# Hybrid decoder step on one core: embedding weights split ahead and a fixed order at the two norm steps

## The chip, the core and the metric

The kernel runs on 1 core of one Trainium2 chip. The metric is device time in microseconds (us). Engines are named as in the profile: PE does matmuls (PEld its weight loads), DVE is the vector engine, ACT the scalar engine, POOL the general engine, SP the queue that starts the transfers.

## The reference, cut to what matters

One layer is computed for 288 positions at once (256 of a prompt, 32 of a sample group), with 2048 features. After the attention and the gated mixer, which the change does not touch, stands this tail:

```python
mix = (ga * a + gb * b) @ w_o
x = x + rms_norm(mix, g_post_mix)
a1, g1 = jnp.split(rms_norm(x, g_pre_ffn) @ w_ffn_in, 2, axis=-1)
f = (jax.nn.silu(a1) * g1) @ w_ffn_out
x = x + rms_norm(f, g_post_ffn)
gate = jax.nn.sigmoid(rms_norm(x, g_ple) @ w_ple_gate)
return x + (p @ w_ple) * gate
```

The two places of the change are the two sums `x + rms_norm(...)`. The small product `p @ w_ple` (256 features in, 2048 out) depends on nothing else in the layer and can be computed anywhere.

## The kernel before

Features lie on the partitions, so a tensor of 2048 features by 288 positions is 16 tiles of 128x288. A product (`product`) goes through groups of 256 output features (two PSUM tiles, t = 0 and 1) and through blocks of four input tiles: one transfer of 512 KB into `wr` (4 buffers, L215), a cast into a high part `wh` on ACT (3 buffers, L218), a subtraction into a low part `wl` on DVE (3 buffers, L219), and then for each input tile and each of the two outputs three matmuls: high by high (L225), high by low (L226), low by high (L227). A block is 24 matmuls. `w_ple` has only two input tiles, so its groups are blocks of 12 matmuls, loaded and split like all others when their turn comes.

At the first place the sequence is: last group of `w_o` (tiles `o`); its squares on ACT (`sq`, L829), summed on POOL except for the last two; a matmul with a constant matrix (`nrm`, L840) that sums over partitions, in plain float32; `rstd_of` (L173 on ACT, L174 to L177 on DVE), which makes 1/sqrt and refines it with a Newton step; `residual`, which for pairs of tiles multiplies by the result (L872), adds to `x1` (L873), casts into the high part of the next input `zh` (L875, ACT), makes its low part `zl` (L876, DVE), squares (L878, ACT) and sums the squares (L880, DVE). After that `w_ffn_in` begins: two groups of its first half (`fa`) and one of its second (`fg`) are woven together, so that three blocks of weights are used side by side. Four groups of `p @ w_ple` (48 matmuls, tiles `le`) lie between `w_o` and `w_ffn_in`, and their copies out of PSUM (L895) are on ACT. The second place is the same with `w_ffn_out` (tiles `f`, `fo`), the other four groups of `w_ple`, and `w_ple_gate` (tiles `pg`, three groups woven) behind it.

The order on each engine is decided when the program is built, by a scheduler that plays the instructions in the order of the code with priorities (`tc.high_priority`); `tc.issue_after(i)` lets an instruction be placed only behind `i`. On the chip every engine then goes through its own row in order and waits on semaphores.

Of the kernel before, what the change touches and what calls it, by code (L numbers as in the profile page):

```python
# [10 lines left out]
F32 = mybir.dt.float32  # L11
# [8 lines left out]
KD = D // 128  # L20
# [88 lines left out]
def tile_hybrid_step(ctx: ExitStack, tc: tile.TileContext, a: dict, o: list):  # L109
# [60 lines left out]

    def rstd_of(dst, ms, tmp):
# [33 lines left out]

    def product(w, c0, ks, part, done, name, of="acc", wide=0):


        accs = [bank([128, T + wide], f"{name}{t}", of) for t in range(2)]
        n = len(ks)  # L210
        for k0 in range(0, n, 4):
            m = min(4, n - k0)
            raw = perm.tile([128, 4, GC], F32, name="wr", bufs=WR)
            r0 = ks[k0] * 128
            nc.sync.dma_start(raw[:, :m], w[r0:r0 + m * 128, c0:c0 + GC].rearrange("(k p) c -> p k c", p=128))  # L215
            wh = perm.tile([128, 4, GC], F32R, name="wh", bufs=3)
            wl = perm.tile([128, 4, GC], F32R, name="wl", tag="wl", bufs=3)
            nc.scalar.copy(wh[:, :m], raw[:, :m])  # L218
            nc.vector.tensor_tensor(wl[:, :m], raw[:, :m], wh[:, :m], ALU.subtract)  # L219
            for i in range(m):  # L220
                k = k0 + i
                x = part(k)
                for t in range(2):
                    c = slice(t * 128, t * 128 + 128)
                    nc.tensor.matmul(accs[t], wh[:, i, c], x[:, :T + wide], start=k == 0, stop=False)  # L225
                    nc.tensor.matmul(accs[t][:, wide:T], wh[:, i, c], x[:, T + wide:], start=False, stop=False)  # L226
                    late["mm"] = nc.tensor.matmul(accs[t][:, :T], wl[:, i, c], x[:, :T], start=False, stop=k == n - 1)  # L227
# [592 lines left out]
    ssq = {}  # L820

    def add_square(key, src, m):

# [4 lines left out]
        q = p_n.tile([128, T], F32, name="sq", bufs=3)  # L828
        nc.scalar.activation(q, src, AF.Square)  # L829
        if m < KD - 2:  # L830
# [3 lines left out]

    def norm_of(key):
        with tc.high_priority():
            ps = bank([128, T], "nrm")
            n = len(ssq[key])
            for i, q in enumerate(ssq[key]):
                nc.tensor.matmul(ps, ones_d, q, start=i == 0, stop=i == n - 1)  # L840
            r = p_n.tile([128, T], F32, name=f"r_{key}", tag="rstd", bufs=3)
            rstd_of(r, ps, p_n.tile([128, T], F32, name=f"rt_{key}", tag="sq", bufs=3))
        return r
# [5 lines left out]
    def wo_done(x, g):  # L849
        for t in range(2):  # L850
            add_square("mo", x[t], 2 * g + t)
        for t in range(2):
            m = 2 * g + t
            nc.scalar.activation(mo_f[:, m], x[t], AF.Copy, scale=g_pm[:, m:m + 1])

    rsqrt_next()
    for g in range(8):
        drain(product(w_o, g * GC, K16, lambda k: mhl[:, k], lambda x, g=g: wo_done(x, g), "o"))

    p_z, end_z = pool("p_z", "right")  # L860
    zhl = p_z.tile([128, KD, 2 * T], F32R, name="zhl")
    zh, zl = zhl[:, :, :T], zhl[:, :, T:]

    def residual(src, rstd, g_next, key):

        last = []
        for m in range(0, KD, 2):
            s = slice(m, m + 2)
            with ExitStack() as st:
                if m >= 4:  # L870
                    st.enter_context(tc.issue_after(last[m - 4].ins))
                nc.vector.tensor_tensor(src[:, s], src[:, s], rstd[:, None, :].to_broadcast([128, 2, T]), ALU.mult)  # L872
                nc.vector.tensor_tensor(x1[:, s], x1[:, s], src[:, s], ALU.add)  # L873
            for k in (m, m + 1):
                nc.scalar.activation(zh[:, k], x1[:, k], AF.Copy, scale=g_next[:, k:k + 1])  # L875
                last.append(nc.vector.scalar_tensor_tensor(zl[:, k], x1[:, k], g_next[:, k:k + 1], zh[:, k],  # L876
                                                           op0=ALU.mult, op1=ALU.subtract))
            nc.scalar.activation(src[:, s], x1[:, s], AF.Square)  # L878
            if m:
                nc.vector.tensor_tensor(src[:, 0:2], src[:, 0:2], src[:, s], ALU.add)  # L880
        ssq[key] = [src[:, 0], src[:, 1]]

# [7 lines left out]
    w_ple = a["w_ple"].rearrange("l k c -> (l k) c")  # L890
    le = p_n.tile([128, KD, T], F32, name="le")

    def le_done(x, g):
        for t in range(2):
            nc.scalar.copy(le[:, 2 * g + t], x[t])  # L895

    def le_products(groups):
        for g in groups:
            drain(product(w_ple, g * GC, [0, 1], lambda k: phl[:, k], lambda x, g=g: le_done(x, g), "le"))

    r1 = norm_of("mo")
    le_products(range(LE))
    residual(mo_f, r1, g_pf, "x1")
# [15 lines left out]
    for half in range(2):  # L919
        pairs = []  # L920
        for g in range(HT // 2):
# [16 lines left out]

            pairs += [product(w_fi, c0, K16, zpart, done_a, "fa"), product(w_fi, FF + c0, K16, zpart, done_g, "fg")]
        if half == 0:  # L940
# [4 lines left out]
        def fo_done(x, g):  # L945
            for t in range(2):
                m = 2 * g + t
                if half == 0:
                    nc.scalar.copy(fo[:, m], x[t])
                else:  # L950
                    nc.vector.tensor_tensor(fo[:, m], fo[:, m], x[t], ALU.add)
                    add_square("fo", fo[:, m], m)
            for m in (2 * g, 2 * g + 1):
                if half:
                    nc.scalar.activation(fo[:, m], fo[:, m], AF.Copy, scale=g_pof[:, m:m + 1])
# [22 lines left out]

    pg = [product(w_pg, g * GC, K16, zpart, lambda x, g=g: pg_done(x, g), "pg") for g in range(8)]
    drain(weave(weave(pg[0], 1.0, pg[1], 1.0), 2.0, pg[2], 1.0))  # L980
# [54 lines left out]
```

## Time and profile before

| | |
|---|---|
| median of 3 runs | 1830.17 us (1830.02 to 1831.29) |
| profiled execution | 1830.38 us, of which the span of instructions 1828.6 us |
| PE busy | 1801.1 us, 98% of the span |
| DVE, ACT busy | 951.3 us (52%), 769.2 us (42%) |
| mean granted TensorE clock | 0.993 of full speed |

The span is what the trace covers. The profiled execution is 1.78 us longer than it, and 0.21 us above the median of the runs.

### The profile page before, as it was taken

How to read it: one execution, taken by the hardware profiler on the slowest of the kernel's cores; microseconds unless marked ns; L12 is line 12 of the kernel's file. 1: busy time of each engine (PE TensorE's matmuls, PEld its weight loads, DVE VectorE, ACT ScalarE, POOL GpSimd, SP SyncE). 2: the span in 40 equal slices, each digit the busy share in tenths (PEclk: the TensorE clock that was granted, in tenths of full speed). 3: DMA queues.
4: the chain of work that ended last, by engine and by line, in shares of the span. 5: the costliest groups of instructions: out<-in, count | busy, mean ns of one | idle time of the engine just before them, and what ended most of it. 6: DMA issues, size and time to landing. Idle time of an engine off the chain costs nothing.

```text
span 1828.6 us, 38398 instructions
## 1 busy us (share of the span) xinstructions
PE 1801.1 (98%) x15818; PEld 1755.9 (96%) x15818; DVE 951.3 (52%) x1361; ACT 769.2 (42%) x1081; POOL 89.7 (5%) x169
## 2 busy tenths in 40 slices
PE   7999999999999999998999999999999999999898
PEld 7999899999999989998999999999999999999898
DVE  7654447554444346535754554443545455444774
ACT  5324455434333344445533333333433343444542
POOL 1010112000000000010000000000000000011000
PEclk9999999999999999999999999999999999999999
DMA  9589999999999986554555555555555555555363
GB/s 343 168 294 359 327 352 332 369 351 362 350 348 347 383 294 202 168 173 139 153 170 162 168 167 162 166 163 169 171 163 171 162 165 170 161 167 162 121 206 112
DMA packets 309136, 414.81 MB, mean 227 GB/s; under 512 B 13120, under 2 KB 273344, under 8 KB 308832
## 3 DMA queue, kind: packets, MB, share of 16 engines
q1 hardware_dynamic: 307728, 409.16, 66.8%
q8 instruction: 124, 2.03, 0.5%
q0 software_dynamic: 944, 2.79, 0.4%
q14 instruction: 52, 0.43, 0.1%
q10 hardware_dynamic: 288, 0.41, 0.1%
HBM read 407.45 MB, written 4.85 MB: 225 GB/s over the span
## 4 chain that ended last, share of the span: by engine, by line
PE 95%; DMA 2%; DVE 1%; ACT 1%; issue 0%; SPq 0%; DVEq 0%; ACTq 0%
PE f L225 6%; PE fa L225 5%; PE fg L225 5%; PE fa L226 5%; PE fa L227 5%; PE fg L226 5%; PE fg L227 5%; PE f L227 5%; PE f L226 5%; PE values L693 3%; PE scores L595 3%; PE pg L225 2%; PE gb L225 2%; PE ga L225 2%; PE pg L226 2%; PE pg L227 2%
## 5 line engine op out<-in xcount | busy, mean ns | idle before, releaser
L219 DVE TENSOR_TENSOR wl<-wr,wh 128x1024 fp32r<-128x1024 f32 (+1 forms) x520 | 624.0, 1201 | 728.7 <-ACT wh L218 721.0
L218 ACT CAST wh<-wr 128x1024 fp32r<-128x1024 f32 (+1 forms) x520 | 535.5, 1030 | 889.3 <-PE f L226 144.0
L225 PE MATMUL f<-dhl,wh 128*128 128x320 f32 x704 | 217.1, 308 | 0.0
L225 PE MATMUL fa<-zhl,wh 128*128 128x288 f32 x704 | 207.9, 297 | 5.4 <-ACT zhl L875 5.4
L226 PE MATMUL fa<-zhl,wh 128*128 128x288 f32 x704 | 208.5, 297 | 0.0
L226 PE MATMUL fg<-zhl,wh 128*128 128x288 f32 x704 | 208.2, 296 | 0.0
L225 PE MATMUL fg<-zhl,wh 128*128 128x288 f32 x704 | 208.0, 296 | 0.0
L227 PE MATMUL fa<-zhl,wl 128*128 128x288 f32 x704 | 207.1, 295 | 0.0
L227 PE MATMUL fg<-zhl,wl 128*128 128x288 f32 x704 | 207.0, 295 | 0.0
L227 PE MATMUL f<-dhl,wl 128*128 128x288 f32 x704 | 207.0, 294 | 0.0
L226 PE MATMUL f<-dhl,wh 128*128 128x256 f32 x704 | 196.9, 280 | 0.0
L225 PEld LDWEIGHTS fa<-zhl,wh 128*128 128x128 f32 x704 | 132.7, 189 | 5.6 <-ACT zhl L875 5.6
L227 PEld LDWEIGHTS fa<-zhl,wl 128*128 128x128 f32 x704 | 133.6, 190 | 0.1
L227 PEld LDWEIGHTS fg<-zhl,wl 128*128 128x128 f32 x704 | 133.2, 190 | 0.0
L226 PEld LDWEIGHTS fa<-zhl,wh 128*128 128x128 f32 x704 | 132.8, 189 | 0.0
L226 PEld LDWEIGHTS f<-dhl,wh 128*128 128x128 f32 x704 | 132.5, 188 | 0.1
L225 PEld LDWEIGHTS fg<-zhl,wh 128*128 128x128 f32 x704 | 132.4, 188 | 0.1
L226 PEld LDWEIGHTS fg<-zhl,wh 128*128 128x128 f32 x704 | 132.3, 188 | 0.1
L227 PEld LDWEIGHTS f<-dhl,wl 128*128 128x128 f32 x704 | 132.2, 188 | 0.1
L225 PEld LDWEIGHTS f<-dhl,wh 128*128 128x128 f32 x704 | 132.0, 188 | 0.0
L225 PE MATMUL pg<-zhl,wh 128*128 128x288 f32 x256 | 75.7, 303 | 5.8 <-ACT zhl L875 5.8
L225 PE MATMUL gb<-hhl,wh 128*128 128x288 f32 x256 | 76.7, 300 | 0.0
(327 smaller groups left out, 3739.9 us busy)
## 6 DMA issues: line engine op xcount, KB each, us to landing
wr<-in_w_ffn_in SPq DMA_DIRECT2D x176, 512.0 KB, 3.7
kt<-in_cache_k SPq DMA_DIRECT2D x128, 512.0 KB, 7.6
vt<-in_cache_v SPq DMA_DIRECT2D x128, 512.0 KB, 6.8
wr<-in_w_in SPq DMA_DIRECT2D x80, 512.0 KB, 7.2
wr<-in_w_ffn_out SPq DMA_DIRECT2D x80, 512.0 KB, 3.5
wr<-in_w_gate SPq DMA_DIRECT2D x64, 512.0 KB, 7.7
wr<-in_w_o SPq DMA_DIRECT2D x32, 512.0 KB, 3.4
wr<-in_w_ple_gate SPq DMA_DIRECT2D x32, 512.0 KB, 3.5
```

Of the source, the lines that this page charges most:

```text
L218: nc.scalar.copy(wh[:, :m], raw[:, :m])
L219: nc.vector.tensor_tensor(wl[:, :m], raw[:, :m], wh[:, :m], ALU.subtract)
L225: nc.tensor.matmul(accs[t], wh[:, i, c], x[:, :T + wide], start=k == 0, stop=False)
L226: nc.tensor.matmul(accs[t][:, wide:T], wh[:, i, c], x[:, T + wide:], start=False, stop=False)
L227: late["mm"] = nc.tensor.matmul(accs[t][:, :T], wl[:, i, c], x[:, :T], start=False, stop=k == n - 1)
L595: i = nc.tensor.matmul(sp[b][32 * g:32 * g + 32, 4 * n:4 * n + 4], Q[:, h2, g, dq], kt[:, :, c:c + 32], start=h2 == 1 and dq == 0, stop=h2 ...
L693: i = nc.tensor.matmul(oa[b][32 * g:32 * g + 8], w[:, n, 32 * g + 8 * part:32 * g + 8 * part + 8], v[:, :, g], start=first and part == 3, ...
```

## The change

It does four things, at both places. The weights of `w_ple` are loaded and split two groups ahead of the end of the product before, into buffers of their own (`leh`, `lel`). The order is written down: one embedding group, then all three `nrm` matmuls together, then the other three groups; squares ahead of the scaled copies; the third woven product's first block held behind the last square. The Newton step writes -2 times the result in one instruction instead of two (`half=False`), and `residual` multiplies by -0.5 in the same instruction that applies it (a SCALAR_TENSOR_TENSOR in place of a TENSOR_TENSOR). The first pair of tiles in `residual` is done as two single tiles. Blocks of two input tiles in `product` are gone through output by output.

```diff
+        if not half:
+            nc.vector.scalar_tensor_tensor(dst, tmp, -3.0, dst, op0=ALU.add, op1=ALU.mult)
+            return
         nc.vector.tensor_scalar(tmp, tmp, -0.5, 1.5, op0=ALU.mult, op1=ALU.add)
         nc.vector.tensor_tensor(dst, dst, tmp, ALU.mult)
...
-            nc.scalar.copy(wh[:, :m], raw[:, :m])
-            nc.vector.tensor_tensor(wl[:, :m], raw[:, :m], wh[:, :m], ALU.subtract)
+            with ExitStack() as st:
+                for i in hold if k0 == 0 else ():
+                    st.enter_context(tc.issue_after(i.ins))
+                nc.scalar.copy(wh[:, :m], raw[:, :m])
+                nc.vector.tensor_tensor(wl[:, :m], raw[:, :m], wh[:, :m], ALU.subtract)
+            for i, t in [(i, t) for i in range(m) for t in range(2)] if m == 4 else [(i, t) for t in range(2) for i in range(m)]:
...
+    def le_weights(groups):
+
         for g in groups:
+            raw = perm.tile([128, 4, GC], F32, name="wr", bufs=WR)[:, :2]
+            nc.sync.dma_start(raw, w_ple[:, g * GC:g * GC + GC].rearrange("(k p) c -> p k c", p=128))
+            h, l = le_w[g] = [p_n.tile([128, 2, GC], F32R, name=f"le{i}", bufs=4) for i in "hl"]
+            nc.scalar.copy(h, raw)
+            nc.vector.tensor_tensor(l, raw, h, ALU.subtract)
...
+    def norm_gap(key, groups):
+
+        groups = list(groups)
+        le_product(groups[0], late["mm"])
+        with tc.issue_after(late["le"].ins):
+            r = norm_of(key, half=False)
+        for g in groups[1:]:
+            le_product(g, late["nrm"])
+        return r
+
+    rsqrt_next()
+    for g in range(8):
+        if g == 6:
+            le_weights(range(LE))
+        drain(product(w_o, g * GC, K16, lambda k: mhl[:, k], lambda x, g=g: wo_done(x, g), "o"))
...
+        last, adds = [], []
+        for m in range(0, KD, 2):
+            s = slice(m, m + 2)
+            for n, i in [(1, m), (1, m + 1)] if m == 0 else [(2, m)]:
+                with ExitStack() as st:
+                    if m >= 4:
+                        st.enter_context(tc.issue_after(last[m - 4].ins))
+                    elif adds:
+                        st.enter_context(tc.issue_after((last[0] if m else adds[-1]).ins))
+                    r = slice(i, i + n)
+                    nc.vector.scalar_tensor_tensor(src[:, r], src[:, r], -0.5, rstd[:, None, :].to_broadcast([128, n, T]),
+                                                   op0=ALU.mult, op1=ALU.mult)
+                    adds.append(nc.vector.tensor_tensor(x1[:, r], x1[:, r], src[:, r], ALU.add))
...
-    r1 = norm_of("mo")
-    le_products(range(LE))
+    r1 = norm_gap("mo", range(LE))
     residual(mo_f, r1, g_pf, "x1")
...
+            hold = [late["sq"]] if half == 0 and g == 1 else []
...
+            if half and g == 6:
+                le_weights(range(LE, 8))
...
-    r4 = norm_of("fo")
-    le_products(range(LE, 8))
+    r4 = norm_gap("fo", range(LE, 8))
```

What this makes of the engines' rows is shown at the first place; the second reads alike. First DVE, from the last weight blocks to the first tile of the residual. Before:

```order
L219 TENSOR_TENSOR wl<-wr,wh 128x512 x4
L219 TENSOR_TENSOR wl<-wr,wh 128x1024
L174 TENSOR_TENSOR rt_mo<-r_mo 128x288
L175 SCALAR_TENSOR_TENSOR rt_mo<-nrm,rt_mo 128x288
L219 TENSOR_TENSOR wl<-wr,wh 128x1024
L176 TENSOR_SCALAR rt_mo<-rt_mo 128x288
L219 TENSOR_TENSOR wl<-wr,wh 128x1024
L177 TENSOR_TENSOR r_mo<-r_mo,rt_mo 128x288
L872 TENSOR_TENSOR mo_f<-mo_f,r_mo 128x576 x2
```

The same stretch of DVE in the changed kernel:

```order
L225 TENSOR_TENSOR wl<-wr,wh 128x1024 x11
L174 TENSOR_TENSOR rt_mo<-r_mo 128x288
L175 SCALAR_TENSOR_TENSOR rt_mo<-nrm,rt_mo 128x288
L177 SCALAR_TENSOR_TENSOR r_mo<-rt_mo,r_mo 128x288
L933 SCALAR_TENSOR_TENSOR mo_f<-mo_f,r_mo 128x288
L935 TENSOR_TENSOR x_10563<-x_10563,mo_f 128x288
L933 SCALAR_TENSOR_TENSOR mo_f<-mo_f,r_mo 128x288
L935 TENSOR_TENSOR x_10563<-x_10563,mo_f 128x288
```

The two subtractions that stood inside the Newton step now stand ahead of it, the four small ones for `w_ple` have moved further up, and the first product and sum are of one tile.

Next PE at the same place; `le_12209` is the second tile of the first embedding group, `le_12234` the first of the second group. Before, the three `nrm` matmuls lay apart, one of them 55 rows ahead of the end of `o` and the others between embedding matmuls:

```order
L227 MATMUL le_12217<-phl,wl 128x288
L840 MATMUL nrm<-sq,ones_d 128x288
L225 MATMUL le_12218<-phl,wh 128x288
L226 MATMUL le_12218<-phl,wh 128x288
L227 MATMUL le_12218<-phl,wl 128x288
L225 MATMUL le_12239<-phl,wh 128x288
L226 MATMUL le_12239<-phl,wh 128x288
L840 MATMUL nrm<-sq,ones_d 128x288
```

In the changed kernel:

```order
L896 MATMUL le_12209<-phl,leh 128x288
L897 MATMUL le_12209<-phl,lel 128x288
L851 MATMUL nrm<-ssq_mo,ones_d 128x288
L851 MATMUL nrm<-sq,ones_d 128x288 x2
L895 MATMUL le_12234<-phl,leh 128x288
L896 MATMUL le_12234<-phl,leh 128x288
```

All three now stand behind the first 12 embedding matmuls, with 36 more behind them.

Last, PE where the first three blocks of `w_ffn_in` (72 matmuls) end and the fourth begins. The tiles `fa_12362`, `fa_12363` belong to the first woven group before (`fa_12363`, `fa_12364` in the changed kernel), the next two numbers to the second, `fg` to the third. Before, the first group is done with its block early (its last use of `wh` is the fifth row here), and the fourth block's first use stands 34 rows below that:

```order
L225 MATMUL fa_12362<-zhl,wh 128x288
L226 MATMUL fa_12362<-zhl,wh 128x288
L227 MATMUL fa_12362<-zhl,wl 128x288
L225 MATMUL fa_12363<-zhl,wh 128x288
L226 MATMUL fa_12363<-zhl,wh 128x288
L227 MATMUL fa_12363<-zhl,wl 128x288
L226 MATMUL fa_12394<-zhl,wh 128x288
L227 MATMUL fa_12394<-zhl,wl 128x288
```

In the changed kernel the three groups go on side by side; the first row here, the 63rd matmul of the stage, is the last use of the first block's `wh`, and the last row is the first use of the fourth block:

```order
L229 MATMUL fa_12364<-zhl,wh 128x288
L230 MATMUL fa_12364<-zhl,wl 128x288
L229 MATMUL fa_12395<-zhl,wh 128x288
L230 MATMUL fa_12395<-zhl,wl 128x288
L229 MATMUL fa_12396<-zhl,wh 128x288
L230 MATMUL fa_12396<-zhl,wl 128x288
L229 MATMUL fg_12427<-zhl,wh 128x288
L230 MATMUL fg_12427<-zhl,wl 128x288
L229 MATMUL fg_12428<-zhl,wh 128x288
L230 MATMUL fg_12428<-zhl,wl 128x288
L228 MATMUL fa_12363<-zhl,wh 128x288
```

The distance between the two has gone from 34 rows to 10. On DVE of the changed kernel the subtraction for that fourth block is the sixth row here:

```order
L938 SCALAR_TENSOR_TENSOR zhl<-x_10563,gains,zhl 128x288
L933 SCALAR_TENSOR_TENSOR mo_f<-mo_f,r_mo 128x576
L938 SCALAR_TENSOR_TENSOR zhl<-x_10563,gains,zhl 128x288
L935 TENSOR_TENSOR x_10563<-x_10563,mo_f 128x576
L942 TENSOR_TENSOR mo_f<-mo_f 128x576
L225 TENSOR_TENSOR wl<-wr,wh 128x1024
L935 TENSOR_TENSOR x_10563<-x_10563,mo_f 128x576
L225 TENSOR_TENSOR wl<-wr,wh 128x1024 x2
```

Ahead of it, from the first L933 on, stand 2 single and 5 paired L933, 2 single and 4 paired L935, 8 L938 (`zl`) and 3 L942 (sums of squares). Before, it stood behind 6 paired L872, 6 paired L873, 8 L876 and 3 L880.

## Rows read from the trace of the kernel before

**Rows 1.** PE's waits of the whole span: us in total, times, longest.

```profile
PE pg L225 <- ACT zhl L875: 5.8, 1, 5.8
PE fa L225 <- ACT zhl L875: 5.4, 1, 5.4
```

**Rows 2.** Timeline of PE, first place: start, length, what, idle before.

```profile
849.71 0.29 PE L225 MATMUL le<-phl,wh 128*128 128x288 f32 x1
...
856.92 0.29 PE L227 MATMUL le<-phl,wl 128*128 128x288 f32 x1
862.58 1.33 PE L225 MATMUL fa<-zhl,wh 128*128 128x288 f32 x4 [5.37 <-ACT zhl L875]
...
865.86 0.31 PE L227 MATMUL fa<-zhl,wl 128*128 128x288 f32 x1
```

**Rows 3.** Windows: length, busy by engine, then PE's granted clock, DMA share, GB/s.

```profile
44.00:48.00 4.00, 3.29 (x14) 3.29 (x14) 3.60 (x4) 1.05 (x1) 0.00 (x0) 0.50 0.51 148
864.00:866.00 2.00, 2.00 (x10) 2.00 (x10) 2.00 (x5) 2.00 (x5) 0.00 (x0) 0.53 0.00 1
```

**Rows 4.** Timeline of PE, second place.

```profile
1704.41 0.29 PE L225 MATMUL le<-phl,wh 128*128 128x288 f32 x1
...
1711.62 0.29 PE L227 MATMUL le<-phl,wl 128*128 128x288 f32 x1
1717.70 1.81 PE L225 MATMUL pg<-zhl,wh 128*128 128x288 f32 x6 [5.78 <-ACT zhl L875]
...
1722.66 0.30 PE L226 MATMUL pg<-zhl,wh 128*128 128x288 f32 x1
```

**Rows 5.** Timeline of ACT, first place.

```profile
849.57 0.41 ACT L829 ACTIVATE sq<-o 128x288 f32<-128x288 f32 x1 [2.35 <-PE o L227]
849.87 0.49 ACT L854 ACTIVATE mo_f<-o,gains 128x288 f32<-128x288 f32 x1
...
853.45 1.05 ACT L218 CAST wh<-wr 128x1024 fp32r<-128x1024 f32 x1 [0.35 <-PE le L226]
854.40 0.39 ACT L895 COPY le<-le 128x288 f32<-128x288 f32 x1
854.69 0.50 ACT L173 ACTIVATE r_mo<-nrm,eps 128x288 f32<-128x288 f32 x1
...
861.99 0.96 ACT L875 ACTIVATE zhl<-x,gains 128x288 fp32r<-128x288 f32 x2 [3.49 <-DVE x L873]
```

**Rows 6.** Timeline of DVE, first place.

```profile
858.24 1.23 DVE L219 TENSOR_TENSOR wl<-wr,wh 128x1024 fp32r<-128x1024 f32 x1
859.38 0.45 DVE L177 TENSOR_TENSOR r_mo<-r_mo,rt_mo 128x288 f32<-128x288 f32 x1
859.86 1.43 DVE L872 TENSOR_TENSOR mo_f<-mo_f,r_mo 128x576 f32<-128x576 f32 x2
861.21 1.42 DVE L873 TENSOR_TENSOR x<-x,mo_f 128x576 f32<-128x576 f32 x2
862.56 0.52 DVE L876 SCALAR_TENSOR_TENSOR zhl<-x,gains,zhl 128x288 fp32r<-128x288 f32 x1
863.00 0.75 DVE L872 TENSOR_TENSOR mo_f<-mo_f,r_mo 128x576 f32<-128x576 f32 x1
```

**Rows 7.** Timeline of PE around the first norm matmul.

```profile
841.92 0.65 PE L840 MATMUL nrm<-ssq_mo,ones_d 128*128 128x288 f32 x2
...
842.54 0.30 PE L225 MATMUL o<-mhl,wh 128*128 128x288 f32 x1
```

**Rows 8.** Groups of DVE by line and form: busy us, mean ns, idle before.

```profile
L876 DVE SCALAR_TENSOR_TENSOR zhl<-x,gains,zhl 128x288 fp32r<-128x288 f32 x32 | 16.0, 510 | 0.0
...
L349 DVE SCALAR_TENSOR_TENSOR p<-s,cm 128x256 f32<-128x256 f32 x4 | 1.7, 413 | 3.2 <-PE s L348 3.2
...
L175 DVE SCALAR_TENSOR_TENSOR rt_mo<-nrm,rt_mo 128x288 f32<-128x288 f32 x1 | 0.5, 458 | 0.0
```

**Rows 9.** Timeline of ACT, second place.

```profile
1705.21 0.45 ACT L829 ACTIVATE sq<-fo 128x288 f32<-128x288 f32 x1
```

More of the change, by code (lines that the diff above doesn't have):

```diff
@@ L1 @@
-from contextlib import ExitStack
+from contextlib import ExitStack, contextmanager
 from itertools import islice
@@ L203, in r0_of, with product @@
         rstd_of(r0, r0p, p_x0.tile([128, T], F32, name="r0t"))
-    def product(w, c0, ks, part, done, name, of="acc", wide=0):
+    def product(w, c0, ks, part, done, name, of="acc", wide=0, hold=()):
         accs = [bank([128, T + wide], f"{name}{t}", of) for t in range(2)]
@@ L820, in tile_hybrid_step, with behind @@
     ssq = {}
+    @contextmanager
+    def behind(keys):
+        with ExitStack() as st:
+            for key in keys:
+                st.enter_context(tc.issue_after(late[key].ins))
+            yield
     def add_square(key, src, m):
@@ L833, in add_square, with norm_of @@
             ssq[key].append(q)
[L835 removed]
+    def norm_of(key, half=True):
         with tc.high_priority():
@@ L839, in norm_of @@
             for i, q in enumerate(ssq[key]):
-                nc.tensor.matmul(ps, ones_d, q, start=i == 0, stop=i == n - 1)
+                late["nrm"] = nc.tensor.matmul(ps, ones_d, q, start=i == 0, stop=i == n - 1)
             r = p_n.tile([128, T], F32, name=f"r_{key}", tag="rstd", bufs=3)
-            rstd_of(r, ps, p_n.tile([128, T], F32, name=f"rt_{key}", tag="sq", bufs=3))
+            rstd_of(r, ps, p_n.tile([128, T], F32, name=f"rt_{key}", tag="sq", bufs=3), half)
         return r
@@ L851, in wo_done @@
             add_square("mo", x[t], 2 * g + t)
[L852 to L881, printed above, removed]
+        with behind(["sq"] if g else []):
+            for t in range(2):
+                m = 2 * g + t
+                nc.scalar.activation(mo_f[:, m], x[t], AF.Copy, scale=g_pm[:, m:m + 1])
     p_f32 = p_n.tile([128, 2, T], F32, name="p_f32")
@@ new lines, in le_product @@
+    def le_product(g, after):
+        with tc.issue_after(after.ins):
+            accs = [bank([128, T], f"le{t}", "acc") for t in range(2)]
+            for t in range(2):
+                c = slice(t * 128, t * 128 + 128)
+                for k in range(2):
+                    h, l = (w[:, k, c] for w in le_w[g])
+                    nc.tensor.matmul(accs[t], h, ph[:, k], start=k == 0, stop=False)
+                    nc.tensor.matmul(accs[t], h, pl[:, k], start=False, stop=False)
+                    late["le"] = nc.tensor.matmul(accs[t], l, ph[:, k], start=False, stop=k == 1)
+                with behind(["sq"]):
+                    nc.scalar.copy(le[:, 2 * g + t], accs[t])
@@ new lines, in tile_hybrid_step, with residual @@
+    zhl = p_z.tile([128, KD, 2 * T], F32R, name="zhl")
+    zh, zl = zhl[:, :, :T], zhl[:, :, T:]
+    def residual(src, rstd, g_next, key):
+        last, adds = [], []
+        for m in range(0, KD, 2):
+            s = slice(m, m + 2)
+            for n, i in [(1, m), (1, m + 1)] if m == 0 else [(2, m)]:
+                with ExitStack() as st:
+                    if m >= 4:
[6 more added lines that the diff above has]
+                    adds.append(nc.vector.tensor_tensor(x1[:, r], x1[:, r], src[:, r], ALU.add))
+                for k in range(i, i + n):
+                    nc.scalar.activation(zh[:, k], x1[:, k], AF.Copy, scale=g_next[:, k:k + 1])
+                    last.append(nc.vector.scalar_tensor_tensor(zl[:, k], x1[:, k], g_next[:, k:k + 1], zh[:, k],
+                                                               op0=ALU.mult, op1=ALU.subtract))
+            nc.scalar.activation(src[:, s], x1[:, s], AF.Square)
+            if m:
+                nc.vector.tensor_tensor(src[:, 0:2], src[:, 0:2], src[:, s], ALU.add)
+        ssq[key] = [src[:, 0], src[:, 1]]
@@ L950, in fo_done @@
                 else:
-                    nc.vector.tensor_tensor(fo[:, m], fo[:, m], x[t], ALU.add)
+                    late["fo"] = nc.vector.tensor_tensor(fo[:, m], fo[:, m], x[t], ALU.add)
                     add_square("fo", fo[:, m], m)
-            for m in (2 * g, 2 * g + 1):
-                if half:
+            for m in (2 * g, 2 * g + 1) if half else ():
+                with behind(["sq"] if g else []):
                     nc.scalar.activation(fo[:, m], fo[:, m], AF.Copy, scale=g_pof[:, m:m + 1])
@@ L977, in pg_done @@
         nc.sync.dma_start(y_o[:, 2 * g:2 * g + 2], x1[:, 2 * g:2 * g + 2])
-    pg = [product(w_pg, g * GC, K16, zpart, lambda x, g=g: pg_done(x, g), "pg") for g in range(8)]
+    pg = [product(w_pg, g * GC, K16, zpart, lambda x, g=g: pg_done(x, g), "pg",
+                  hold=[late["sq"], late["fo"]] if g == 2 else []) for g in range(8)]
     drain(weave(weave(pg[0], 1.0, pg[1], 1.0), 2.0, pg[2], 1.0))
```

25 lines of the change are left out of this document (9 added, 16 removed).

## The prediction

> **What bounds the kernel now.** I read the list of PE's waits first. PE is busy almost the whole span, so only what PE loses counts. In the part of the program that the change touches the list has two entries: one wait of 5.4 us ahead of the first `fa` matmul and one of 5.8 us ahead of the first `pg` matmul, both for the cast that makes `zh` [rows 1]. They are the two norm steps.
>
> Then the timelines of PE at these places. In the first, the last embedding matmul starts at 856.92 and the first of `w_ffn_in` at 862.58. The matmuls after it start 0.24 us apart instead of 0.13, until 865.86 [rows 2]. The window there has a granted clock of 0.53, so PE ran almost wholly at the lower of its two levels, 1.2 GHz [rows 3]. From 856.92 to 865.86 the trace has 14 starts in 8.94 us; at the usual 0.132 us (47 embedding starts and two norm matmuls of 0.49 us between 849.71 and 856.92 [rows 2]) they take 1.85. Lost: 7.1 us. In the second place 21 starts take from 1711.62 to 1722.66, 11.04 us, in place of 2.77 [rows 4]. Lost: 8.3 us. Together 15.4 us, 0.84% of the run; no edit here can bring more than that.
>
> What PE waits for is read in the timelines of ACT and DVE. The last subtraction ahead of the end of the Newton step runs 858.24 to 859.38, then come the end of the step, two products and two sums on pairs of tiles (0.67 us each), and at 861.99 the cast of the first tile [rows 5, 6]. PE starts 0.59 us later [rows 2]. So DVE's queue ends the wait, and in it two subtractions of weights, 1.14 us each, that the norm doesn't need.
>
> **The change, first place, step by step.** I play the new order of the three engines with the spacings of these rows, on the time axis of before.
>
> *PE.* A norm matmul costs 842.54 − 841.92 less one product matmul, 0.49 us [rows 7]. One of the three moves from inside `o` to behind it, so `o` ends 0.49 earlier and the embedding starts at 849.22. 12 of its matmuls (1.58), three norm matmuls (1.47) and 36 more (4.75) leave PE free at 857.02. The sum of PE's work is unchanged.
>
> *ACT.* One starts the next about 0.10 before the end of the former: a square takes 0.30, a scaled copy 0.39, a cast of a block 0.95, a copy 0.29 [rows 5]. The first square starts at 849.57 − 0.49 = 849.08, the second at 849.48 when its tile is done; then two scaled copies, two casts, two copies, and the reciprocal root at 853.04, done at 853.54. The norm matmuls, at 850.80 to 852.27, are not late for it.
>
> *DVE.* The second of the two casts ends at 852.56; its subtraction follows the first one's and leaves DVE free at 853.93, just behind the root. Then instructions that wait for each other, 0.48 to 0.49 apart [rows 6]: three of the Newton step, the product of one tile at 855.40, its sum at 855.89, done at 856.34. The cast on ACT stands behind the seventh embedding copy (its matmul 856.10, the copy 856.49) and starts at 856.78. With the 0.59 of before, PE starts at 857.37 and has waited 0.35 in place of 5.4. A wait of this length leaves the clock where it is.
>
> *What is late next.* From 857.37 on 72 matmuls take 9.5 us, to 866.87. Three waits lie there. (a) The fourth weight block can be cast only when the 63rd matmul, the last on the first block, is done: 865.55 + 0.39 = 865.94, plus 1.05, so PE gets it at 867.04, a wait of 0.17. (b) The next cast is 0.95 behind, PE has four matmuls to cover it, 0.42 more. (c) Eight matmuls on, at 868.5, PE wants the low part of that block. On DVE its subtraction stands behind 1.7 us of single tiles, 5 paired products and 4 paired sums (0.67 each), 8 low parts (0.43) and 3 sums of squares (0.67), 13.4 us with 0.2 for two short waits; 855.40 + 13.4 = 868.8, plus 1.23 and the signal: 870.06. PE waits 1.55. The place loses 2.5 us in place of 7.1. Before, wait (c) was hidden by the slow clock: by the same prices that subtraction stood 13.5 us behind the first product (6 paired products, 6 paired sums, 8 low parts, 3 sums of squares), but PE at 1.2 GHz came late to it.
>
> The price of the new product, SCALAR_TENSOR_TENSOR with an immediate factor, is not in the trace for these sizes. From below: 0.458 for 288 elements and 0.413 for 256 with an immediate factor, one source in PSUM, the second of them with a repeated operand as here; these are what TENSOR_TENSOR costs, so 0.46 and 0.75 for a pair. From above: 0.510 with both sources in SBUF and a factor for each partition, so 0.51 and 0.81 [rows 8]. I take the lower, because of the immediate factor. The upper adds 0.06 to each pair, and with about 7 pairs' worth in the two waits of a place some 0.4 us for each, 0.8 in all. The trace has both sources in SBUF at 0.510 for 288 elements, that is at full rate [rows 8]. The Trainium skill has a rule that speaks against the edit (Vector Engine (DVE) Microarchitecture Reference, Points that are easy to get wrong): this shape of instruction with two non-bf16 SBUF sources "halves throughput". By the row the sum gives 1820.6 to 1821.4, by the rule the 1829.0 of the third rival; the trace does not agree with the rule.
>
> **Second place.** Here the square of the first of the last two tiles comes 0.80 behind the first embedding matmul (1705.21 against 1704.41) [rows 4, 9], where in the first place it comes 0.14 ahead (849.57 against 849.71) [rows 2, 5], because the tile first takes two additions on DVE. That is 0.94 later, of which 0.2 goes into time in which DVE and the cast were held by other things before. First wait 0.35 + 0.75 = 1.1, then the same 2.15 for (a) to (c): 3.25 us in place of 8.3.
>
> The embedding's early loads and splits cost PE nothing: 4 transfers of 256 KB, 4 casts and 4 subtractions of half blocks are as many as before and move into a product in which ACT and DVE wait for PE (the square at 849.57 had 2.35 us of idle ahead of it [rows 5]). Without that cover they would show as up to 4 x (0.5 + 0.6) = 4.4 us, by half of a block's cast and subtraction [rows 5, 6]. The output-by-output order of small blocks changes no count; nothing.
>
> **Sum.** Lost before 15.4, after 2.5 + 3.25 = 5.75; gain 9.6 us. The profiled execution, 1830.38 with 1828.6 of span and 1.78 around it, would become 1820.8, and the median, 0.2 lower, 1820.6 us: 0.53% faster. Of the 15.4, 11.5 are the two waits, start to start, and 3.9 the clock; 1.45 of the waits stays and 4.3 are new.
>
> **Rivals.**
> - *The clock falls at the new waits.* (a) to (c) are 2.15 us within 3.2. For it: between 44 and 48 us PE was busy 3.29 of 4.00 and the clock was 0.50 throughout [rows 3]; against it: PE is busy about 0.8 of the time around these waits and almost all of it ahead. It would give back what the clock cost before, 1.6 and 2.3 us (7.1 less 5.5 of idle, 8.3 less 5.9), more or less: 1824.5. Chance 0.11.
> - *No new waits.* If the casts or DVE are a little earlier than played, (a) to (c) shrink, to nothing at best: 15.4 − 1.45 = 14.0, 1816.2; half of them, 1818.4. For it: the wait (c) hangs on 13.4 us of DVE work to within some 10%. Chance 0.10.
> - *Half rate.* The new product reads two float32 sources from SBUF; if such an instruction streamed at half the rate, 288 elements would take 0.75 and a pair 1.35 (the 0.15 of fixed cost and twice the 0.30 that 288 more elements add, 0.45 to 0.75 [rows 6]). With 7 pairs' worth for each place, 2 x 7 x 0.6 = 8.4 us more: 1829.0, no change that can be seen. Against it: L876 also reads two float32 tiles from SBUF and takes 0.510 for 288 [rows 8]. Chance 0.03.
> - *Slower.* The same place with a higher price: the product is on the path to the first cast and stands ahead of each wait (c). The saved 9.6 us are spent when a pair costs 9.6 / 14 = 0.69 more, 1.44 us. At twice the lower row or a little over, 1.55, it would be 1831.8, and over 0.2% slower from 1.7 on. Nothing in the rows speaks for it. Chance 0.04.
> - *It doesn't do what it says.* A queue that I have not played rightly (the transfers, the held blocks) puts a wait of some 4 us back in each place: 1828.6. Chance 0.05.
>
> **How the numbers follow.** The forecast, 1819 to 1822.5, has 0.67. A measurement of this kernel can tell about 0.2%, 3.7 us, from no change. Faster by more: forecast, clock and no new waits, 0.88. Within: half rate, the last rival and part of the slower one, 0.09. Slower: 0.03. The range 1817.0 to 1825.0 holds the forecast, the upper price, the clock rival and half of the waits gone, about 0.83.
>
> **What would show it.** The first `fa` matmul starts 0.2 to 0.6 us behind the last embedding matmul's slot, the first `pg` one 0.8 to 1.4; the granted clock stays at 1.00 in both stages; new entries in PE's waits for `wh` and `wl` (L224, L225) of about 0.6 and 1.5 us in each place; L933 at 0.46 and 0.75. Wrong would be: L933 over 0.9 for a pair; a clock of 0.5 behind the new waits; a first wait over 2 us.

## The result, and the profile after

| | before | after |
|---|---|---|
| median of the runs beside each other | 1830.32 us (6 runs, 1829.96 to 1831.29) | 1819.84 us (6 runs, 1819.00 to 1821.75) |
| profiled execution, its span | 1830.38, 1828.6 us | 1820.68, 1818.9 us |
| mean granted clock | 0.993 | 0.996 |

The ratio is 0.9944, with a 95% interval of 0.9932 to 0.9955: 0.56% faster. Forecast were 1820.6 us and 0.53%.

First the list of PE's waits of the changed kernel (us in total, times, longest):

```profile
...
PE pg L230 <- DVE wl L225: 1.2, 1, 1.2
PE fa L230 <- DVE wl L225: 1.2, 1, 1.2
...
PE pg L228 <- ACT zhl L937: 0.9, 1, 0.9
...
PE fg L228 <- ACT wh L224: 0.2, 1, 0.2
PE pg L228 <- ACT wh L224: 0.2, 1, 0.2
```

The two waits of 5.4 and 5.8 us [rows 1] have become one of 0.9 us; the first `fa` matmul's is too short for the list. New are a wait for a low part `wl` and one for a cast `wh` in each place.

The timeline of PE at the first place (start, length, what, idle before):

```profile
857.31 0.29 PE L897 MATMUL le<-phl,lel 128*128 128x288 f32 x1
857.74 0.79 PE L228 MATMUL fa<-zhl,wh 128*128 128x288 f32 x4
...
867.25 0.29 PE L230 MATMUL fg<-zhl,wl 128*128 128x288 f32 x1
867.55 0.40 PE L228 MATMUL fa<-zhl,wh 128*128 128x288 f32 x1
867.79 0.29 PE L229 MATMUL fa<-zhl,wh 128*128 128x288 f32 x1
...
868.05 0.29 PE L229 MATMUL fa<-zhl,wh 128*128 128x288 f32 x1
868.50 0.40 PE L228 MATMUL fg<-zhl,wh 128*128 128x288 f32 x1 [0.15 <-ACT wh L224]
868.74 0.29 PE L229 MATMUL fg<-zhl,wh 128*128 128x288 f32 x1
...
869.00 0.30 PE L229 MATMUL fg<-zhl,wh 128*128 128x288 f32 x1
870.49 0.53 PE L230 MATMUL fa<-zhl,wl 128*128 128x288 f32 x2 [1.19 <-DVE wl L225]
```

A wait is read from start to start, less the usual 0.13 us; the idle time in brackets is smaller, because a matmul counts as busy until it drains. The first wait is 857.74 − 857.31 − 0.13 = 0.30 us. Then come the three that the prediction calls (a), for the cast of the fourth weight block, 0.17 us, (b), for the next cast, 0.32, and (c), for the fourth block's low part, 1.36. The same in the second place:

```profile
1707.12 0.29 PE L897 MATMUL le<-phl,lel 128*128 128x288 f32 x1
1708.33 1.06 PE L228 MATMUL pg<-zhl,wh 128*128 128x288 f32 x6 [0.92 <-ACT zhl L937]
...
1719.55 0.29 PE L229 MATMUL pg<-zhl,wh 128*128 128x288 f32 x1
1721.07 0.53 PE L230 MATMUL pg<-zhl,wl 128*128 128x288 f32 x2 [1.23 <-DVE wl L225]
```

Here the first wait is 1.08 and (c) 1.39; (a) and (b) are 0.12 and 0.32. Windows of both stages, to be held against [rows 3]:

```profile
864.00:866.00 2.00, 2.00 (x17) 2.00 (x16) 2.00 (x5) 1.54 (x3) 0.00 (x0) 1.00 0.00 0
868.00:872.00 4.00, 2.66 (x18) 2.18 (x17) 4.00 (x5) 3.69 (x7) 0.00 (x0) 1.00 0.08 15
...
1719.00:1722.00 3.00, 1.73 (x11) 1.50 (x12) 3.00 (x5) 2.65 (x5) 0.00 (x0) 1.00 0.00 0
```

The clock is 1.00 throughout, at the higher of its two levels, and DVE (third of the busy times) is busy without a break while PE waits. What DVE does is in its timeline:

```profile
855.81 0.46 DVE L933 SCALAR_TENSOR_TENSOR mo_f<-mo_f,r_mo 128x288 f32<-128x288 f32 x1
856.30 0.46 DVE L935 TENSOR_TENSOR x<-x,mo_f 128x288 f32<-128x288 f32 x1
...
868.54 0.76 DVE L942 TENSOR_TENSOR mo_f<-mo_f 128x576 f32<-128x576 f32 x1
869.21 1.22 DVE L225 TENSOR_TENSOR wl<-wr,wh 128x1024 fp32r<-128x1024 f32 x1
```

The low part of the fourth block begins 13.40 us behind the first product (13.4 forecast), though its cast, the first of three in this row of ACT's timeline, was done in time for the matmul of 867.55:

```profile
866.44 2.95 ACT L224 CAST wh<-wr 128x1024 fp32r<-128x1024 f32 x3 [0.63 <-ACT mo_f L940]
```

Last the price of the new product, from the groups of DVE by form (busy us, mean ns):

```profile
L938 DVE SCALAR_TENSOR_TENSOR zhl<-x,gains,zhl 128x288 fp32r<-128x288 f32 x32 | 16.2, 518 | 0.1
...
L933 DVE SCALAR_TENSOR_TENSOR mo_f<-mo_f,r_mo 128x576 f32<-128x576 f32 x7 | 5.2, 755 | 0.0
...
L933 DVE SCALAR_TENSOR_TENSOR mo_f<-mo_f,r_mo 128x288 f32<-128x288 f32 x2 | 0.9, 454 | 0.0
...
L177 DVE SCALAR_TENSOR_TENSOR r_mo<-rt_mo,r_mo 128x288 f32<-128x288 f32 x1 | 0.5, 457 | 0.0
```

It is the lower of the two prices, that of TENSOR_TENSOR.

### The profile page after: what moved, and what is told of

Same layout as the page of the kernel before. It is cut to its first block, busy times and chain, and to the rows that moved or that the text cites. A ratio compares the mean times of both kernels' runs of the same rounds, so it can differ in the third digit from the quotient of the medians.

```text
span 1818.9 us, 38387 instructions
## 1 busy us (share of the span) xinstructions
PE 1798.5 (99%) x15818; PEld 1752.1 (96%) x15818; DVE 951.9 (52%) x1363; ACT 769.2 (42%) x1081; POOL 90.6 (5%) x169
## 3 DMA queue, kind: packets, MB, share of 16 engines
q8 instruction: 124, 2.03, 0.5%
## 4 chain that ended last, share of the span: by engine, by line
PE 94%; DVE 3%; DMA 1%; SPq 1%; issue 1%; ACT 1%; DVEq 0%; ACTq 0%
PE f L228 6%; PE f L230 5%; PE fg L228 5%; PE fg L230 5%; PE fg L229 5%; PE fa L230 5%; PE fa L228 5%; PE fa L229 5%; PE f L229 5%; PE values L696 3%; PE scores L598 3%; PE gb L228 2%; PE ga L228 2%; PE gb L230 2%; PE o L228 2%; PE o L230 2%
## 5 line engine op out<-in xcount | busy, mean ns | idle before, releaser
L225 DVE TENSOR_TENSOR wl<-wr,wh 128x1024 fp32r<-128x1024 f32 x512 | 618.8, 1209 | 708.2 <-ACT wh L224 704.4
L224 ACT CAST wh<-wr 128x1024 fp32r<-128x1024 f32 x512 | 530.9, 1038 | 881.0 <-PE f L229 140.4
L230 PEld LDWEIGHTS f<-dhl,wl 128*128 128x128 f32 x704 | 132.2, 188 | 0.0
L228 PE MATMUL ga<-hhl,wh 128*128 128x288 f32 x256 | 76.5, 299 | 0.0
```

## The experiments

**The theory under test.** DVE's row runs without a break from the norm to the low part of the fourth weight block, and where that ends is where each place ends; PE's waits and its clock only divide the time up to there. **Rivals**: the clock's loss is a cost of its own; single edits carry the gain, each with its own share; DVE's work is mostly covered.

**How they are measured.** The part of the program ahead of `w_o` differs from profile to profile (first `o` matmul between 745.9 and 751.3 us), by more than most effects here. So beside median and ratio I give the *stretch*, from the start of the first `o` matmul to that of the last `pg` matmul in PE's timeline, and for kernels with the order of the changed one the two *places*: from the second embedding matmul behind the norm matmuls to the first matmul with the low part of the fourth block. All in us. The early split alone is built on the kernel before, all others on the changed one. Stretch and places are from one profiled execution of each kernel; the changed kernel's two profiles and that of the late split agree to 0.03 us, while the executions of one kernel spread over up to 5 us, so that medians alone do not tell effects of 1 us apart.

| kernel | median | ratio to before, interval | stretch | places |
|---|---|---|---|---|
| before | 1830.32 | | 1075.08 | |
| changed | 1819.84 | 0.9944 (0.9932 to 0.9955) | 1064.94 | 17.67, 18.45 |
| changed, again | 1819.93 | 0.9946 (0.9932 to 0.9959) | 1064.91 | 17.67, 18.45 |
| before, early split alone | 1826.08 | 0.9976 (0.9967 to 0.9986) | 1070.71 | |
| late split | 1819.76 | 0.9943 (0.9926 to 0.9960) | 1064.92 | 17.67, 18.45 |
| order alone | 1821.99 | 0.9959 (0.9944 to 0.9974) | 1066.60 | 18.45, 19.17 |
| begun with a pair | 1822.03 | 0.9954 (0.9938 to 0.9971) | 1067.69 | 18.46, 18.83 |
| full Newton step | 1820.39 | 0.9950 (0.9933 to 0.9966) | 1064.71 | 18.46, 18.74 |
| norm later | 1828.07 | 0.9988 (0.9979 to 0.9997) | 1072.97 | 21.92, 22.83 |
| norm later, PE kept busy | 1827.81 | 0.9985 (0.9976 to 0.9994) | 1073.83 | 21.93, 22.84 |
| pairs twice | 1827.01 | 0.9981 (0.9972 to 0.9990) | 1072.39 | 16.81, 17.60 |
| own buffer for the fourth block | 1816.23 | 0.9923 (0.9909 to 0.9936) | 1061.10 | |

**Norm later, and norm later with PE kept busy.** The first puts nine empty instructions between the Newton step and the residual:

```diff
             r = norm_of(key, half=False)
+            for _ in range(9):
+                nc.vector.tensor_tensor(r, r, r, ALU.max)
```

> The changed kernel, but nine instructions that change nothing (the result of the Newton step, the larger of itself and itself) stand on DVE between the Newton step and the residual at each place: 9 x 0.49 = 4.4 us later. The first waits become about 4.5 and 5.3 us, and the clock should fall behind them as in the kernel before. Theory (DVE's row sets the end of each place, and the slow clock only takes time in which PE would have waited for the low part of a weight block): all moves by 4.4 us and by nothing else, 8.6 to 8.8 us more than the changed kernel: span near 1827.6. Rival (the clock's loss comes on top): about 1.6 us more for each place, span near 1831.

The second has these and, behind the embedding matmuls, 33 matmuls whose results nobody uses:

```diff
+        with tc.issue_after(late["le"].ins):
+            spare = bank([128, T], "spare")
+            for _ in range(33):
+                nc.tensor.matmul(spare, ph[:, 0, :128], ph[:, 0], start=True, stop=True)
```

> The kernel of the run with the nine instructions, but 33 matmuls whose results nobody uses stand on PE behind the last embedding matmul of each place, so that PE is busy while it waits. The clock stays at full. Theory (DVE's row sets the end): the same time as without the 33 matmuls, within 0.5 us, span near 1827.6; in place of the slow clock the waits for the fourth block show, 0.2, 0.4 and 1.8 us for each place. Rival (the clock's loss comes on top of the waits, so that keeping it pays): 3 us less than without the 33 matmuls.

The second place in both, PE's timeline and a window, first with PE idle in the wait:

```profile
1705.46 0.29 PE L896 MATMUL le<-phl,leh 128*128 128x288 f32 x1
...
1728.28 0.53 PE L230 MATMUL pg<-zhl,wl 128*128 128x288 f32 x2 [0.28 <-DVE wl L225]
```

```profile
1715.40:1719.30 3.90, 3.90 (x16) 3.90 (x17) 3.90 (x8) 1.90 (x4) 0.00 (x0) 0.50 0.00 0
```

Then with PE kept busy:

```profile
1705.95 0.29 PE L896 MATMUL le<-phl,leh 128*128 128x288 f32 x1
...
1728.79 0.53 PE L230 MATMUL pg<-zhl,wl 128*128 128x288 f32 x2 [1.42 <-DVE wl L225]
```

```profile
1715.40:1719.30 3.90, 3.43 (x26) 3.43 (x27) 3.87 (x8) 1.82 (x4) 0.00 (x0) 1.00 0.02 4
```

With the clock at 0.50 PE begins the low part after 22.83 us and has waited 0.44 for it, start to start; with the clock at 1.00 it begins after 22.84 and has waited 1.58. At the first place it is 21.92 and 21.93. The slow clock costs nothing here: it takes time that the wait (c) would have taken. Both places move by 4.3 and 4.4 us against the changed kernel, as the nine instructions do. The rival, 3 us between the two, is out. The stretch of the second kernel is 0.9 longer, for something nobody expected, in the window behind its wait (c) at the first place:

```profile
874.80:878.00 3.20, 3.20 (x16) 3.20 (x15) 3.20 (x5) 1.14 (x3) 0.00 (x0) 0.50 0.86 258
```

The clock has fallen behind a wait of 1.5 us (starts 872.08 and 873.75), and here, past that matmul, nothing hides it. 13 starts are 0.24 us apart instead of 0.13, 1.4 us, of which 0.6 are won back by a closer spacing elsewhere (last section).

**Pairs twice.** Each paired product is done a second time into a spare tile:

```diff
-                    nc.vector.scalar_tensor_tensor(src[:, r], src[:, r], -0.5, rstd[:, None, :].to_broadcast([128, n, T]),
+                    for dst in [again] * (n == 2) + [src[:, r]]:
+                        nc.vector.scalar_tensor_tensor(dst, src[:, r], -0.5, rstd[:, None, :].to_broadcast([128, n, T]),
```

> The changed kernel, but each of the seven paired products in a residual is done twice, once more into a spare tile, as if its price were 0.67 us higher (the distance of two such instructions in DVE's row); the two single products stay. Theory: the price is felt in full ahead of the low part of the fourth block and by what stands behind it: five pairs for each place by the prediction's count, 2 x 5 x 0.67 = 6.7 us more than the changed kernel: span near 1825.6, median near 1826.5. Rival (DVE's row is covered by PE's work for the most part): at most 1 us more, span below 1820.

The stretch is 7.45 us longer and the median 7.2 us, with 6.7 expected: DVE's row is not covered. But the time is not lost where it was expected. As built, the subtraction for the fourth block has moved up DVE's row:

```profile
859.06 0.46 DVE L935 SCALAR_TENSOR_TENSOR mo_f<-mo_f,r_mo 128x288 f32<-128x288 f32 x1
...
871.59 1.22 DVE L225 TENSOR_TENSOR wl<-wr,wh 128x1024 fp32r<-128x1024 f32 x1
```

Ahead of it stand seven paired products, the doubled ones counted, three paired sums, six low parts and two sums of squares, where the changed kernel has five, four, eight and three. It begins 12.53 us behind the first product instead of 13.40, and both places are 0.9 shorter. The time is lost behind them: in place of one wait (c) there are several for `wl`, for the cast of later tiles and for their low parts. So this run shows that time added to DVE's row is lost on PE, but it does not test the count of five pairs: that 7.45 is near 6.7 does not confirm it. (The profiled execution, 1831.37 us, has a start 3.2 us later than the changed kernel's and is no measure; the other ten end between 1826.12 and 1827.74.)

**Own buffer for the fourth block.** At each place its two parts take buffers that the embedding weights have left, so its cast needs no matmul of the first block to end, and both are placed behind the low part of the fourth tile:

```diff
+            if k0 == own:
+                wh, wl = [p_n.tile([128, 4, GC], F32R, name=f"le{i}", bufs=2) for i in "hl"]
...
+                if k0 == own:
+                    st.enter_context(tc.issue_after(late["zl"][3].ins))
                 nc.scalar.copy(wh[:, :m], raw[:, :m])
```

> The changed kernel, but at each place the fourth weight block gets the buffers that the embedding weights leave (high and low part), and is cast and split once the low part of the fourth tile of the residual is made. Theory (DVE's queue ends each place by the low part of the fourth block): the waits (a) to (c) go, measured 0.17 + 0.32 + 1.35 at the first place and 0.12 + 0.32 + 1.39 at the second, with 0.3 more in each place for the slower restarts behind them; some 0.3 us comes back in each place as a wait for a low part of the input. 3.8 us less than the changed kernel: span near 1815.1, median near 1816.0; the first waits 0.3 and 1.1 stay. Rival (the subtraction is only moved, DVE has the same work, so the wait goes to the next low parts of the input): less than 1 us gained, span above 1818.

DVE's and PE's timelines of this kernel:

```profile
862.69 1.22 DVE L228 TENSOR_TENSOR lel<-wr,leh 128x1024 fp32r<-128x1024 f32 x1
```

```profile
867.14 0.30 PE L233 MATMUL fg<-zhl,wl 128*128 128x288 f32 x1
867.27 0.43 PE L231 MATMUL fa<-zhl,leh 128*128 128x288 f32 x2
867.54 0.29 PE L232 MATMUL fa<-zhl,leh 128*128 128x288 f32 x1
867.67 0.29 PE L233 MATMUL fa<-zhl,lel 128*128 128x288 f32 x1
```

The subtraction runs 6.5 us earlier, and the fourth block begins 0.13 us behind the third's last matmul: waits (a) to (c) are gone in both places. The stretch is 3.84 us shorter, 3.8 expected, and the median 1816.23. This kernel beats both.

**Before, with the early split alone.** Only `le_weights` and its buffers are added to the kernel before (and `p` is loaded ahead of `w_o`, as in the changed one):

```diff
+        if g == 6:
+            le_weights(range(LE))
         drain(product(w_o, g * GC, K16, lambda k: mhl[:, k], lambda x, g=g: wo_done(x, g), "o"))
```

> The kernel before with one part of the change alone: embedding weights loaded and split two groups ahead into buffers of their own; the order of the norm matmuls and squares, the Newton step and the residual are those of before. The two subtractions no longer stand inside the Newton step, but in the order as built the last norm matmul lies behind 36 embedding matmuls at the first place and behind all 48 at the second. First place: root at 855.2, four steps of Newton, two paired products and a sum, first matmul at about 860.0 instead of 862.6; second place: nothing lies behind the last norm matmul, and the chain of 0.5 + 1.8 + 2.0 + 0.6 us stays as a wait of over 5 us. Theory (each place moves with its chain): 2.5 + 0.8 us gained, median near 1827.0. Rival (the weights in the chain were the whole trouble): 7 us or more gained, below 1823.

Its list of waits:

```profile
PE pg L225 <- ACT zhl L897: 5.2, 1, 5.2
PE fa L225 <- ACT zhl L897: 2.8, 1, 2.8
...
PE fg L225 <- ACT wh L218: 1.3, 1, 1.3
```

4.4 us of the stretch are gained, 3.3 expected; some 1.4 of it is a closer spacing of matmuls far from the places (last section). The first place gains 2.6 (2.5 expected), and some 0.4 is left for the second (0.8 expected). Its wait moves little: there the last norm matmul still lies behind all 48 embedding matmuls.

**Late split.** The reverse, the changed kernel with its embedding weights split where they are used:

```diff
         groups = list(groups)
+        le_weights(groups)
...
-        if g == 6:
-            le_weights(range(LE))
```

> The changed kernel, but the embedding weights are loaded and split at the norm step in the order of the code, not two groups ahead; own buffers, order and hold stay. The build's order puts their casts and subtractions still ahead of the last group's end. Theory (what counts is that no cast or subtraction of weights stands in the norm's chain; how far ahead they are does not): no change, within 0.5 us of 1819.8. Rival (the early loads carry the gain): 3 us or more lost.

The stretch is the same to 0.02 us and both places to 0.01: beside the order, the early split adds nothing.

**Begun with a pair.** The single tiles are undone:

```diff
-            for n, i in [(1, m), (1, m + 1)] if m == 0 else [(2, m)]:
+            for n, i in [(2, m)]:
```

> The changed kernel, but the residual begins with a pair of tiles as before, not with two single ones. Product and sum of the first tile take 0.67 instead of 0.49 each, 0.36 us; in this kernel's order the cast of the first tile stands behind the eighth embedding copy instead of the seventh at the first place, some 0.4 more there. Theory (one chain from the norm to the low part of the fourth block): DVE's next instruction needs that cast, so all of DVE's row moves with it, though it has 0.62 us less work: 0.8 at the first place and 0.4 at the second, 1.2 us more than the changed kernel, median near 1821.0. Rival (the sum of DVE's work alone decides): 0.6 us less for each place, median near 1818.6.

The places are 0.79 and 0.38 longer (0.8 and 0.4 expected), though DVE has less work. So it is not the sum of work that counts but the chain: what stands behind the first cast in DVE's row moves with it. The stretch is 2.75 longer, because 1.5 us more were lost behind the second place, where a low-part wait of 2.05 us (starts 1718.80 and 1720.98) was followed by this window:

```profile
1722.30:1725.60 3.30, 3.30 (x16) 3.30 (x15) 3.30 (x6) 1.47 (x3) 0.00 (x0) 0.50 0.88 287
```

**Full Newton step.** Newton step and product as before:

```diff
-            r = norm_of(key, half=False)
+            r = norm_of(key)
...
-                    nc.vector.scalar_tensor_tensor(src[:, r], src[:, r], -0.5, rstd[:, None, :].to_broadcast([128, n, T]),
-                                                   op0=ALU.mult, op1=ALU.mult)
+                    nc.vector.tensor_tensor(src[:, r], src[:, r], rstd[:, None, :].to_broadcast([128, n, T]), ALU.mult)
```

> The changed kernel with the Newton step and the product of before (four instructions instead of three; TENSOR_TENSOR instead of the product with a factor). One instruction of 0.31 us more on the chain, 0.35 with its distance; at the first place the cast again falls behind the eighth embedding copy, 0.4 more. Theory: 1.1 us more than the changed kernel in all, median near 1820.9; the pairs cost the same 0.75. Rival (the new product has a higher price than the trace shows, through contention): no change or less time.

The places are 0.79 and 0.29 longer, 1.08 together (1.1 expected), and a paired TENSOR_TENSOR takes 0.752 us, as much as the product with a factor:

```profile
L933 DVE TENSOR_TENSOR mo_f<-mo_f,r_mo 128x576 f32<-128x576 f32 x7 | 5.2, 752 | 0.0
```

Yet the stretch is not longer: 1.3 us are won elsewhere, by the closer spacing (last section). The run alone would have misled; the places settle it.

**Order alone.** The last three edits at once: late split, full Newton step and product of before, a pair first.

```diff
+        le_weights(groups)
...
-            r = norm_of(key, half=False)
+            r = norm_of(key)
...
-            for n, i in [(1, m), (1, m + 1)] if m == 0 else [(2, m)]:
+            for n, i in [(2, m)]:
```

> The order of the changed kernel alone: Newton step, product and first pair of the residual are those of before, and the embedding weights are loaded and split at the norm step. Theory: the order carries nearly all of the gain. At the first place the cast of the first tile waits for the eighth embedding copy anyway, so the longer chain costs the same 0.8 us as each undone edit alone; at the second place 0.3 + 0.4 add up: 1.5 us more than the changed kernel, median near 1821.3; with a low-part wait of some 2.2 us at the second place the clock may fall behind it as in the kernel with the pair, 1.5 us more, 1822.9. Rival (the four edits each carry a share): 1825 or more.

The places are 0.78 and 0.72 longer, as expected: at the first the two edits do not add, since the first cast there waits for the eighth embedding copy in either case. The stretch is 1.66 longer (1.5 expected), so the order alone brings 8.5 of the 10.1 us. Its clock did not fall behind a wait (c) of 2.03 us, as long as that of the kernel begun with a pair. The second place there:

```profile
1701.15 0.29 PE L896 MATMUL le<-phl,leh 128*128 128x288 f32 x1
...
1720.32 0.53 PE L230 MATMUL pg<-zhl,wl 128*128 128x288 f32 x2 [1.87 <-DVE wl L225]
```

**The changed kernel again**, with no edit.

> The changed kernel once more, with more executions. Two other kernels showed a stretch of 14 to 30 matmuls at the lower clock behind a low-part wait of 1.5 to 2 us, which the changed kernel's profile does not have. Theory (the changed kernel's waits of 1.4 us leave the clock alone, as in its first profile): stretch from the first matmul of o to the last of pg 1064.9 us again, executions spread only by the start of the program, median 1819 to 1820.5. Rival (the clock falls behind them in some executions): a profile with starts 0.24 us apart behind a wait, stretch 1.5 to 3 us longer, or executions that cluster that much apart.

Both places are the same to 0.01 us, the clock stays, and the stretch is 1064.91. (The expectation speaks of 14 to 30 matmuls at the lower clock in two other kernels; it is 14 starts in each.) What spreads the executions over 2.7 us is not seen in these two profiles.

## Why the prediction was right

**The bound.** That PE lost some 15 us in two waits and behind them, and that DVE's row ended them, is borne out. The stretch is 10.1 us shorter. By starts and gaps as in the forecast, 15.4 lost before less 5.9 after, it is 9.5; the other 0.6 lies outside the two places (0.06 ahead of the first, 0.28 between them, 0.24 behind the second) and stays unassigned. The medians lie 10.5 apart; that is 0.4 more, less than the executions of one kernel differ by.

**The terms.** First waits 0.30 and 1.08 (0.35 and 1.1 forecast). Wait (a) 0.17 and 0.12 (0.17), (b) 0.32 (0.42), (c) 1.36 and 1.39 (1.55). Not foreseen: behind each of the four waits of a place the second start comes 0.24 us after the first instead of 0.13, 0.43 for a place. The sums are 2.6 and 3.3, with 2.5 and 3.25 forecast; the terms mis-sized are (b) and (c), by 0.3 for a place, the missing one is the restart, and they nearly cancel. By the theory that is no luck. What the prediction fixed is the end of DVE's row: its 870.06 stands 17.66 us behind the second embedding matmul that follows the norm matmuls (849.22 + 1.58 + 1.47 + 0.13 = 852.40), and the place measures 17.67. A restart ahead of that end comes out of (b) and (c); only the one behind (c), 0.11, is added, and the sums are off by that 0.1.

**The price of the product.** 0.454 and 0.755, the lower bound, so the choice by the immediate factor was right. The rival of half rate, 1.35 for a pair, is out; the Trainium skill's sentence that this shape with two non-bf16 sources in SBUF "halves throughput" (Vector Engine (DVE) Microarchitecture Reference, Points that are easy to get wrong) does not hold for this instruction: both products read two float32 tiles from SBUF at the rate of TENSOR_TENSOR, 0.752 for the same pair.

**The slower rival.** Its mechanism is real, its price not: 0.67 more for each pair cost 7.45 us of stretch. That is 11 us for each us of price where the two single products are left out; the prediction's 14, whose seven pairs' worth for a place had some 1.3 for them, would give 11.4. As the order of DVE's row differs in that kernel, the agreement supports the size and does not test the count.

**The clock.** The step "before, wait (c) was hidden by the slow clock" is shown by the two kernels with the later norm. It also means that most of the 3.9 us which the prediction booked as won from the clock are no gain of their own: up to the low part of the fourth block they were exchanged for (a) to (c), 3.7 us with no restarts counted. Not all: in the kernel before, PE came late to that low part in the second place. DVE and PE there:

```profile
1728.47 1.21 DVE L219 TENSOR_TENSOR wl<-wr,wh 128x1024 fp32r<-128x1024 f32 x1
```

```profile
1730.62 0.43 PE L227 MATMUL pg<-zhl,wl 128*128 128x288 f32 x2
```

The subtraction ended at 1729.69, and the matmul started 0.9 us later; in the changed kernel it is 0.06 (870.43 and 870.49). At the first place it was 0.2 (874.58 and 874.82). So of the two slow stretches before, some 1 us was a loss of its own, nearly all at the second place, and the theory that DVE's row ends each place is not exact for that one.

The rival that the clock falls at the new waits did not come true in the changed kernel (two profiles), but did in two of its neighbours, at 1.4 and 1.5 us each. What decides it is open: behind a wait (c) of 1.4 it stayed, behind one of 1.5 it fell and behind one of 1.6 in the same kernel it stayed, behind 2.05 it fell in one kernel and behind 2.03 it stayed in another, and in the early split alone it stayed behind a first wait of 3.0. I tried nothing that tells these apart.

**Where the gain came from.** The prediction played all edits together. The runs show that the order (the norm matmuls together behind the first embedding group, squares ahead of copies, no subtraction in the Newton step) carries 8.5 us, the shorter chain 1.7, the early split nothing on top. The parts of the order were not tried one by one; the early split alone, which takes the subtractions out of the Newton step and leaves the rest, gave 3.0 without the closer spacing.

**No new waits.** This rival was wrong as to the change, and right as to what is to be had: with another buffer the waits go, and the time is 1816.23 (1816.2 forecast for it).

## What to carry to other kernels

When a long wait is removed, look for the queue that ended it and go down its row to the next thing that the bounding engine wants from it: here 13.4 us of residual work stood ahead of one subtraction of weights, and the new wait could be computed from the old trace. A slow clock behind a wait is not always a loss; where the next wait lies within it, winning the clock back only shows that wait. And when effects are a thousandth of the run, measure the stretch that the change touches, from one matmul to another, not the whole.

## What the runs showed of the hardware that was not expected

- **Restart.** In both places the matmul that ends a wait is followed by the next 0.24 us later instead of 0.13, at a granted clock of 1.00 (867.55 and 867.79, 868.50 and 868.74), whatever the wait's length (0.12 to 1.4 us, and the same behind the 3.0 of the early split alone). It is the spacing that the windows at 0.50 show; why it appears here is open.
- **Spacing.** The 2112 `w_ffn_in` matmuls of the second half take 279.90 us from first to last start in the changed kernel and 279.11 in the one with the full Newton step, 132.6 against 132.2 ns each, evenly over the whole stretch, with no wait and the same rows; in the first half the last 1700 spacings take 225.41 and 224.77. The profiled executions fall on the one value or the other, that of the kernel with the norm later on one in each half. Whether it goes with the kernel or with the execution was not tried, beyond the changed kernel, whose two profiles agree. The cause is open.
- **A pointer and an immediate.** The same instruction on 288 elements from SBUF takes 0.518 us with a factor for each partition (L938) and 0.454 with an immediate one (L933). The two also write different types, fp32r and f32, so that the factor alone is not shown to be the cause.
